# A gate-scaled one-hot matrix made by compare-then-multiply on VectorE, without ScalarE

## The chip, the cores and the metric

The kernel runs on one core of one Trainium2 chip. The core has five engines, each with a queue of its own that it works off in order: TensorE (PE in the profile, with PEld for its weight loads), VectorE (DVE), ScalarE (ACT), GpSimd (POOL) and SyncE (SP, which issues most DMAs). The metric is the device time of one execution in microseconds (us), the median of several runs.

## The reference: what is computed

The program is one layer of a hybrid decoder: a state-space branch, a dilated attention branch and a memory attention branch over 1024 tokens of width 1024, merged and added to the residual. Behind them stands a retrieval layer (PEER), and the change lies there. For each token, 8 heads choose 16 experts each out of 16384 = 128 x 128, so a token has 128 chosen experts with a softmax gate each:

```python
idx = jnp.take_along_axis(cidx, pos, axis=-1)
gate = jax.nn.softmax(top, axis=-1)
u = expert_down[ib]
act = jax.nn.gelu(jnp.einsum('bld,blhkd->blhk', hb, u), approximate=False)
coef = (gb * act.astype(F32)).astype(hb.dtype)
vv = expert_up[ib]
return jnp.einsum('blhk,blhkd->bld', coef, vv)
```

## The kernel before

The 1024 tokens are 8 tiles of 128. Four of them (`GATHERED`: 0, 1, 4, 5) fetch the rows of the chosen experts one by one: GpSimd gathers a row per token, VectorE takes its dot product with the token (L1109), and TensorE sums the rows of the second table (L1154). The other four (`DENSE`: 2, 3, 6, 7) compute all 16384 experts with matmuls and multiply the result by a matrix W of gates that is zero for an expert that a token did not choose. W is parked in HBM as `w_park` and read back as `wbig` tiles in the dense part.

`gates_of` builds W, four tokens in a step, 32 steps for a tile. An expert's number is split into a high part (number >> 7) and a low part. The two parts and the gate are transposed, so that `sl[:, n, t]` holds for token t, on partition j, what its j-th choice has: n = 0 the high part, n = 1 the low part, n = 2 the gate. For the four tokens of a step, VectorE compares a row of 0 to 127 (`iota`) with the low parts (`o2`, L1221) and with the high parts (`og`, L1222), each as one operation of 128x512. ScalarE multiplies each token's 128x128 block of `og` by that token's gates (L1224, four operations). In `product`, one step later, TensorE multiplies the two blocks for each token (L172, four matmuls of 128x128, held in program order by `pinned`), and ScalarE copies the result from PSUM into a stage tile (L1207), which SP writes to `w_park` after every four steps (L1210).

Two stretches of the program run this. The first does tiles 2 and 3 as a side job (`early_gates`) beside the front part of the second half: there `og` and `o2` are `work` tiles and the PSUM tile is called `s`. The second does tiles 6 and 7 (`gates` in `dense`) beside `begin`, which computes 23 slices of the dense hidden layer ahead, each with 24 matmuls, two ScalarE casts (`whi`, L244) and two VectorE subtractions (`wlo`, L245). There the one-hot tiles lie in a `wbig` buffer (`hots`, four steps deep) and the PSUM tile is called `mm`; `coef` is the name of the tile that holds `sl`. Beside both, VectorE does the dot products of the gathers (L1109) and the choice of experts (`top16` and `two_heads`, L965 to L1008). After the second stretch come five more slices of the hidden layer, pinned behind it, and then the dense products of the remaining program.

The order of the work is set by the order in which the generators are advanced (by a running estimate of TensorE time), and then by the tile framework's scheduler, which sorts each engine's queue by priority and by its own idea of when an operand is ready. So a change of an operation's kind and engine can also move its neighbours.

Of the kernel before, what the change touches and what calls it, by code (L numbers as in the profile page):

```python
# [14 lines left out]
AF = mybir.ActivationFunctionType  # L15
ALU = mybir.AluOpType
# [86 lines left out]
def tile_hybrid_block(ctx: ExitStack, tc: tile.TileContext, keep_d, cst_d, vec_d, row_d, pos_d, xT_d, memT_d, w_in, w_mem_kv,  # L103
                      w_ssd_br, w_dil_br, w_mem_br, w_out, w_query, subk_d, down_d, up_d, downT_d, out):
    nc = tc.nc
# [44 lines left out]
    def gtiny(n, dt, tag, bufs):  # L150
        return new(gsmall, [P, n], dt, tag, bufs)[:, :n]
# [8 lines left out]
    def ps(tag=None):  # L160
        turn[0] += 1
        return bank(tag if tag and psums[tag][1] else "t" if turn[0] % 2 and psums["t"][1] else "s")
# [7 lines left out]
    def mm(o, lhsT, rhs, **kw):  # L170
        cost(o, 4 if rhs.dtype == F32 else 1)
        return nc.tensor.matmul(o, lhsT, rhs, **kw)  # L172

    def tr(o, x, i):
        cost(o, 2)
        nc.tensor.transpose(o, x, i)  # L176
# [6 lines left out]
    iota = keep[:, K_IOTA:K_IOTA + P]  # L183
# [914 lines left out]
    def pinned(ins):  # L1098

        tc.keep_in_program_order(ins)  # L1100
# [83 lines left out]
    def gates_of(d, expert, gate, alloc, ps, hot, stage_of):  # L1184

        t, slots = alloc(), alloc()
        ei = gtiny(P, I32, "ei", 1)
        nc.vector.tensor_copy(ei, expert)
        nc.vector.tensor_scalar(out=ei, in0=ei, scalar1=7, scalar2=None, op0=ALU.logical_shift_right)
        nc.vector.tensor_copy(t[:, 0:128], ei)  # L1190
        nc.vector.scalar_tensor_tensor(t[:, 128:256], t[:, 0:128], -128.0, expert, op0=ALU.mult, op1=ALU.add)
        tp = ps()
        for n, x in enumerate((t[:, 0:128], t[:, 128:256], gate)):
            tr(tp[:, n * P:(n + 1) * P], x, ident)
        nc.scalar.copy(slots[:, 0:384], tp[:, 0:384])
        yield
        sl = slots[:, 0:384].rearrange("p (n t) -> p n t", n=3)
        iota4 = iota.unsqueeze(1).to_broadcast([P, 4, P])
        todo = []

        def product():
            (o2, og), stage, b, t4 = todo.pop(0)
            pw = ps()
            for tq in range(4):
                pinned(mm(pw[:, tq * P:(tq + 1) * P], o2[:, tq, :], og[:, tq, :], start=True, stop=True))
            for c0, n, part in stage:
                nc.scalar.copy(part[:, :, t4 * 4:t4 * 4 + 4], pw.rearrange("p (t c) -> p c t", t=4)[:, c0:c0 + n, :])  # L1207
            if t4 == WT // 4 - 1:
                for c0, n, part in stage:
                    nc.sync.dma_start(w_park[d * (P // WT) + b, :, c0:c0 + n, :], part)  # L1210

        for b in range(P // WT):
            stage = stage_of(b)
            for t4 in range(WT // 4):
                t0 = b * WT + t4 * 4

                def of(n):
                    return sl[:, n, t0:t0 + 4].unsqueeze(2).to_broadcast([P, 4, P])

                o2, og = (hot(n).rearrange("p (t c) -> p t c", t=4) for n in range(2))  # L1220
                nc.vector.tensor_tensor(out=o2, in0=iota4, in1=of(1), op=ALU.is_equal)  # L1221
                nc.vector.tensor_tensor(out=og, in0=iota4, in1=of(0), op=ALU.is_equal)  # L1222
                for tq in range(4):
                    nc.scalar.activation(out=og[:, tq, :], in_=og[:, tq, :], func=AF.Copy, scale=sl[:, 2, t0 + tq:t0 + tq + 1])  # L1224
                todo.append(((o2, og), stage, b, t4))
                if len(todo) == 2:
                    product()
                yield
        product()

    def dense(hn, dpool):
# [54 lines left out]
        def gates():  # L1286
            stages = new(dpool, [P, 2, P, WT], F32, "wbig", 2)
            hots = new(dpool, [P, 8, NW], F32, "wbig", 2)
            step = [0]

            def hot(n):
                step[0] += n == 0
                return hots[:, 2 * (step[0] % 4) + n, :]

            for d, tt in enumerate(DENSE):
                if tt >= NT:
                    while tt not in routed:
                        next(sides[-1][0])
                        yield
                    yield from gates_of(d, *routed[tt], dslab, big_ps, hot, lambda b: [(0, P, stages[:, b % 2])])  # L1300
# [92 lines left out]
    def early_gates():  # L1393
        def stage_of(b):
            return [(32 * k, 32, work().rearrange("p (c t) -> p c t", t=WT)) for k in range(4)]

        for d, tt in enumerate(DENSE):
            if tt < NT:
                while tt not in routed:
                    yield IDLE  # L1400
                for _ in gates_of(d, *routed[tt], work, ps, lambda n: work(), stage_of):
                    yield paces["gates"]
# [90 lines left out]
```

## Time and profile before

| | us |
|---|---|
| median of 3 runs | 4039.79 |
| lowest and highest run | 4023.14, 4045.42 |
| the profiled execution, its own time | 4024.51 |
| its span, first to last instruction | 4022.6 |
| first stretch of gate steps (tiles 2 and 3) | 1666 to 2042 |
| second stretch of gate steps (tiles 6 and 7) | 2236 to 2411 |

The profile shows one execution. An engine is busy while an instruction of it runs; instructions of one engine overlap a little, so the distance from one start to the next is what an instruction takes from its queue, and its duration is longer. The idle time of an engine is put down to what it waited for last. PE is the busiest engine over the span, and the stretches differ: the table of stretches further down gives the busy time of each engine in each.

### The profile page before, as it was taken

How to read it: one execution, taken by the hardware profiler on the slowest of the kernel's cores; microseconds unless marked ns; L12 is line 12 of the kernel's file. 1: busy time of each engine (PE TensorE's matmuls, PEld its weight loads, DVE VectorE, ACT ScalarE, POOL GpSimd, SP SyncE). 2: the span in 40 equal slices, each digit the busy share in tenths (PEclk: the TensorE clock that was granted, in tenths of full speed). 3: DMA queues.
4: the chain of work that ended last, by engine and by line, in shares of the span. 5: the costliest groups of instructions: out<-in, count | busy, mean ns of one | idle time of the engine just before them, and what ended most of it. 6: DMA issues, size and time to landing. Idle time of an engine off the chain costs nothing.

```text
span 4022.6 us, 54006 instructions
## 1 busy us (share of the span) xinstructions
PE 3743.0 (93%) x17838; PEld 2805.3 (70%) x17838; DVE 2759.6 (69%) x7131; ACT 1502.5 (37%) x3326; POOL 1200.8 (30%) x1081
## 2 busy tenths in 40 slices
PE   8989999999989998898898888989999999999997
PEld 5766888877766786666566665667777777777664
DVE  5763454559988768898769997876667666666432
ACT  4543344343533333455542682222223222222221
POOL 0000000000123323344344323434443345444444
PEclk9989999999999988999999998999999999999999
DMA  3233233444556756788788878989998889889898
GB/s 96 75 96 90 76 108 110 137 148 136 152 173 211 231 172 229 256 312 303 278 321 313 308 259 298 317 273 318 318 319 291 290 306 324 304 310 314 302 323 312
DMA packets 452824, 956.28 MB, mean 238 GB/s; under 512 B 44480, under 2 KB 173248, under 8 KB 450496
## 3 DMA queue, kind: packets, MB, share of 16 engines
q0 software_dynamic: 147456, 536.94, 38.3%
q1 hardware_dynamic: 305088, 415.90, 31.9%
q8 instruction: 140, 2.29, 0.2%
q14 instruction: 140, 1.15, 0.1%
HBM read 882.94 MB, written 69.73 MB: 237 GB/s over the span
## 4 chain that ended last, share of the span: by engine, by line
PE 62%; DMA 13%; DVE 12%; issue 8%; POOL 2%; ACT 2%; SPq 0%; POOLq 0%; DVEq 0%; ACTq 0%
PE mm L172 36%; PE s L172 18%; PE up L1154 4%; DMA wraw<-in_downT_dram 3%; PE t L172 3%; DMA rowd<-in_down_dram,ids 3%; DVE rowd L1109 2%; DVE wlo L245 2%; DMA wraw<-in_up_dram 2%; POOL rowd L1115 1%; PE s L176 1%; DMA rowd<-in_up_dram,ids 1%; DMA slab<-y_park 1%; DMA rowu<-in_up_dram,ids 1%; DVE junk L1007 1%
## 5 line engine op out<-in xcount | busy, mean ns | idle before, releaser
L244 ACT CAST whi<-wraw 128x512 fp32r<-128x512 f32 (+2 forms) x1002 | 613.6, 613 | 1701.3 <-PE mm L172 775.7
L245 DVE TENSOR_TENSOR wlo<-wraw,whi 128x512 fp32r<-128x512 f32 (+2 forms) x1002 | 678.3, 679 | 763.3 <-ACT whi L244 671.1
L1115 POOL DMA_INDIRECT rowd<-in_down_dram,ids x512 | 603.5, 1179 | 1227.2 <-DVE act L1109 809.6
L172 PE MATMUL mm<-uslab,whi 128*128 128x512 f32 x2240 | 735.3, 406 | 0.3 <-ACT uslab L244 0.2
L172 PE MATMUL mm<-whi,coef 128*128 128x512 f32 x2048 | 677.6, 401 | 32.1 <-DVE acc L1345 17.1
L172 PE MATMUL s<-uslab,whi 128*128 128x512 f32 (+1 forms) x2080 | 664.2, 401 | 36.3 <-ACT whi L244 29.1
L1109 DVE CUSTOM_DVE_ANT_0 rowd<-rowd,rowd 128x1024 f32<-128x1024 f32 x512 | 616.9, 1219 | 111.3 <-DMA rowd<-in_down_dram,ids 107.2
L1168 POOL DMA_INDIRECT rowu<-in_up_dram,ids x448 | 514.7, 1149 | 575.5 <-PE up L1154 452.8
L172 PEld LDWEIGHTS s<-uslab,whi 128*128 128x128 f32 (+1 forms) x2080 | 390.2, 190 | 164.0 <-issue 37.4
L172 PEld LDWEIGHTS mm<-whi,coef 128*128 128x128 f32 x2048 | 389.8, 190 | 156.7 <-issue 45.4
L172 PEld LDWEIGHTS mm<-uslab,whi 128*128 128x128 f32 x2240 | 419.7, 192 | 93.6 <-issue 10.8
L172 PE MATMUL mm<-uslab,wlo 128*128 128x512 f32 x1120 | 450.5, 405 | 11.1 <-DVE wlo L245 10.9
L172 PE MATMUL s<-uslab,wlo 128*128 128x512 f32 (+1 forms) x1040 | 414.6, 399 | 8.4 <-DVE wlo L245 8.4
L172 PE MATMUL mm<-wlo,coef 128*128 128x512 f32 x1024 | 408.3, 399 | 0.0
L172 PE MATMUL mm<-slab,whi 128*128 128x512 f32 x768 | 253.6, 408 | 21.0 <-DVE slab L245 8.7
L172 PEld LDWEIGHTS mm<-uslab,wlo 128*128 128x128 f32 x1120 | 213.8, 191 | 63.0 <-DVE wlo L245 14.1
L1154 PE MATMUL up<-rowu,one_col 128*32 128x512 f32 x1792 | 225.5, 613 | 20.2 <-DMA rowu<-in_up_dram,ids 19.7
L527 POOL COPY slab<-halo 128x3 f32<-128x3 f32 x32 | 12.2, 385 | 766.6 <-DVE posf L1002 750.1
L172 PEld LDWEIGHTS s<-uslab,wlo 128*128 128x128 f32 (+1 forms) x1040 | 197.3, 190 | 60.4 <-DVE wlo L245 15.7
L172 PE MATMUL mm<-whi,uslab 128*128 128x512 f32 (+1 forms) x768 | 236.1, 388 | 0.0
L172 PEld LDWEIGHTS mm<-wlo,coef 128*128 128x128 f32 x1024 | 195.3, 191 | 46.8 <-issue 1.7
L172 PEld LDWEIGHTS mm<-slab,whi 128*128 128x128 f32 x768 | 143.1, 191 | 61.8 <-DVE slab L245 12.9
(314 smaller groups left out, 5035.8 us busy)
## 6 DMA issues: line engine op xcount, KB each, us to landing
wraw<-in_downT_dram SPq DMA_DIRECT2D x256, 256.0 KB
wraw<-in_up_dram SPq DMA_DIRECT2D x256, 256.0 KB
wraw<-in_w_in_dram SPq DMA_DIRECT2D x152, 256.0 KB
wbig<-w_park SPq DMA_DIRECT2D x16, 2048.0 KB
wraw<-in_w_in_dram SPq DMA_DIRECT2D x160, 128.0 KB
slab<-y_park SPq DMA_DIRECT2D x64, 256.0 KB
wraw<-in_w_query_dram SPq DMA_DIRECT2D x64, 256.0 KB
w_park<-work SPq DMA_DIRECT2D x64, 256.0 KB
```

The costliest lines, as they stand in the source:

```text
L172: return nc.tensor.matmul(o, lhsT, rhs, **kw)
L176: nc.tensor.transpose(o, x, i)
L244: nc.scalar.copy(hi, src)
L245: nc.vector.tensor_tensor(out=lo, in0=src, in1=hi.bitcast(F32), op=ALU.subtract)
L527: nc.gpsimd.tensor_copy(r[:, 0:3], halo[:, f, :])
L1007: nc.vector.tensor_tensor(out=junk, in0=junk, in1=d3[:, h, :].unsqueeze(1).to_broadcast([P, 16, NCAND]), op=ALU.mult)
L1109: pinned(nc.vector.tensor_tensor_reduce(out=r, in0=r, in1=hn, scale=1.0, scalar=0.0, op0=ALU.mult, op1=ALU.add, accum_out=act[:, j:j + 1]))
L1115: nc.gpsimd.indirect_dma_start(out=r, out_offset=None, in_=down_d, in_offset=bass.IndirectOffsetOnAxis(ap=ids[:, j:j + 1], axis=0))
L1154: pinned(nc.tensor.matmul(up[32 * q:32 * q + 32, hh * 512:(hh + 1) * 512], z[:, q, 31 - n:63 - n], four[q][:, hh * 512:(hh + 1) * 512], st ...
L1168: nc.gpsimd.indirect_dma_start(out=r, out_offset=None, in_=up_d, in_offset=bass.IndirectOffsetOnAxis(ap=ids[:, 128 + t:129 + t], axis=0))
```

## The change

The compare of the high part is no longer made for four tokens at once and then scaled on ScalarE. For each token, one VectorE operation takes `iota`, compares it with the token's high parts (one value for each partition) and multiplies the outcome by the token's gates (again one value for each partition).

```diff
                 nc.vector.tensor_tensor(out=o2, in0=iota4, in1=of(1), op=ALU.is_equal)
-                nc.vector.tensor_tensor(out=og, in0=iota4, in1=of(0), op=ALU.is_equal)
                 for tq in range(4):
-                    nc.scalar.activation(out=og[:, tq, :], in_=og[:, tq, :], func=AF.Copy, scale=sl[:, 2, t0 + tq:t0 + tq + 1])
+                    nc.vector.tensor_scalar(out=og[:, tq, :], in0=iota, scalar1=sl[:, 0, t0 + tq:t0 + tq + 1],
+                                            scalar2=sl[:, 2, t0 + tq:t0 + tq + 1], op0=ALU.is_equal, op1=ALU.mult)
```

Over the program this takes 512 operations of 128x128 from ScalarE and 128 of 128x512 from VectorE, and adds 512 of 128x128 to VectorE.

The end of VectorE's queue in the second stretch, before (rows without numbers at their start; `keep` holds `iota`, `top` and `cand` belong to the choice of experts, `wlo` to the hidden layer):

```order
L1221 TENSOR_TENSOR wbig_19631<-keep,coef_21666 128x512
L966 MAX_INDEX pos_22183<-top_21057,cand_22127 128x8
L1222 TENSOR_TENSOR wbig_19631<-keep,coef_21666 128x512
L967 MATCH_REPLACE cand_22127<-top_21057,cand_22127 128x50
L245 TENSOR_TENSOR wlo_22257<-wraw_22254,whi_22256 128x512
L968 MAX top_21057<-cand_22127 128x8
L245 TENSOR_TENSOR wlo_22275<-wraw_22272,whi_22274 128x512
```

The same place in the changed kernel:

```order
L1221 TENSOR_TENSOR wbig_19567<-keep,coef_21570 128x512
L966 MAX_INDEX pos_22059<-top_20977,cand_22006 128x8
L1223 TENSOR_SCALAR wbig_19567<-keep,coef_21570 128x128
L967 MATCH_REPLACE cand_22006<-top_20977,cand_22006 128x50
L1223 TENSOR_SCALAR wbig_19567<-keep,coef_21570 128x128
L968 MAX top_20977<-cand_22006 128x8
L1223 TENSOR_SCALAR wbig_19567<-keep,coef_21570 128x128
L969 MAX_INDEX pos_22059<-top_20977,cand_22006 128x8
L1223 TENSOR_SCALAR wbig_19567<-keep,coef_21570 128x128
L245 TENSOR_TENSOR wlo_22129<-wraw_22126,whi_22128 128x512
L245 TENSOR_TENSOR wlo_22147<-wraw_22144,whi_22146 128x512
```

One operation of a step has become four, and the small operations that stood between the steps now stand between the four as well. Between the first and the last gate operation of this stretch the queue holds the same other work in both kernels, but for one pass of `top16` whose last pieces cross the end (27 against 28 of L967 to L969).

The end of ScalarE's queue in the second stretch, before:

```order
L1207 COPY wbig_19630<-mm_22223 128x128x4
L1224 ACTIVATE wbig_19631<-wbig_19631,coef_21666 128x128 x4
L1207 COPY wbig_19630<-mm_22240 128x128x4
L1207 COPY wbig_19630<-mm_22246 128x128x4
L1075 ACT_TABLE_LOAD
```

And in the changed kernel:

```order
L1207 COPY wbig_19566<-mm_22096 128x128x4
L1207 COPY wbig_19566<-mm_22112 128x128x4
L1207 COPY wbig_19566<-mm_22118 128x128x4
L244 CAST whi_22196<-wraw_22194 128x512
L1075 ACT_TABLE_LOAD
```

Nothing but the copies out of PSUM is left of the gate steps on ScalarE.

VectorE's queue in the first stretch, at the 18th step, before (`rowd` is a gathered row, `slab` and `wlo` belong to the front part):

```order
L1221 TENSOR_TENSOR work_15872<-keep,work_14893 128x512
L966 MAX_INDEX idxs_15795<-vals_15794,sc_15792 128x8
L1222 TENSOR_TENSOR work_15873<-keep,work_14893 128x512
L245 TENSOR_TENSOR slab_15836<-slab_15710,slab_15835 128x512
L967 MATCH_REPLACE sc_15792<-vals_15794,sc_15792 128x128
```

And in the changed kernel:

```order
L1221 TENSOR_TENSOR work_15855<-keep,work_14893 128x512
L966 MAX_INDEX idxs_15779<-vals_15778,sc_15776 128x8
L1223 TENSOR_SCALAR work_15856<-keep,work_14893 128x128
L967 MATCH_REPLACE sc_15776<-vals_15778,sc_15776 128x128
L1223 TENSOR_SCALAR work_15856<-keep,work_14893 128x128
L968 MAX vals_15778<-sc_15776 128x8
L1223 TENSOR_SCALAR work_15856<-keep,work_14893 128x128
L969 MAX_INDEX idxs_15779<-vals_15778,sc_15776 128x8
L1109 ISA rowd_15666,act_13895<-rowd_15666,rowd_13893 128x1024
L1109 ISA act_13895 128x1
L1223 TENSOR_SCALAR work_15856<-keep,work_14893 128x128
```

Here the fourth token's operation has come to stand behind a dot product of a gathered row. The order of TensorE's matmuls moves by a few places in both stretches, and the last matmul of the second stretch keeps its place among the others.

## Rows read from the trace of the kernel before

**Rows 1.** Busy time and share of the span of each engine, from the page.

```profile
PE 3743.0 (93%) x17838; PEld 2805.3 (70%) x17838; DVE 2759.6 (69%) x7131; ACT 1502.5 (37%) x3326; POOL 1200.8 (30%) x1081
```

**Rows 2.** Busy time by stretch: stretch, its length, then each engine's busy us.

```profile
core 0: us, PE busy (x) PEld busy (x) DVE busy (x) ACT busy (x) POOL busy (x), PEclk, DMA share, GB/s
1666.00:1850.00 184.00, 161.98 (x852) 120.94 (x851) 157.92 (x424) 98.82 (x324) 71.99 (x63) 0.97 0.88 308
1850.00:2042.00 192.00, 165.35 (x859) 117.02 (x859) 138.87 (x249) 111.14 (x343) 79.76 (x66) 0.96 0.82 296
2160.00:2236.00 76.00, 68.21 (x305) 49.09 (x298) 74.50 (x296) 21.51 (x36) 35.11 (x28) 0.96 0.85 301
2236.00:2408.00 172.00, 152.80 (x895) 121.48 (x893) 167.13 (x538) 129.31 (x353) 52.27 (x38) 0.99 0.78 281
2408.00:2600.00 192.00, 165.50 (x731) 120.54 (x732) 154.87 (x423) 51.18 (x90) 76.70 (x63) 0.92 0.89 304
2600.00:3700.00 1100.00, 1063.71 (x4918) 794.34 (x4917) 724.45 (x1283) 308.72 (x518) 481.97 (x420) 0.98 0.89 306
```

**Rows 3.** Groups by line and shape: count, busy us, mean ns, idle before and releasers.

```profile
L172 PE MATMUL s<-work,work 128*128 128x128 f32 x576 | 84.8, 288 | 17.7 <-ACT work L1224 15.2 <-DVE work L890 2.3
L172 PE MATMUL mm<-wbig 128*128 128x128 f32 x512 | 78.0, 300 | 16.9 <-ACT wbig L1224 15.6 <-issue 1.1
L1224 ACT ACTIVATE wbig<-wbig,coef 128x128 f32<-128x128 f32 x256 | 82.2, 395 | 10.1 <-DVE wbig L1222 9.2 <-ACT whi L244 0.6
L1222 DVE TENSOR_TENSOR wbig<-keep,coef 128x512 f32<-128x512 f32 x64 | 43.6, 681 | 0.0
```

**Rows 4.** Timeline of the second stretch's last steps: start us, duration us, engine, operation.

```profile
2388.39 0.68 DVE L1221 TENSOR_TENSOR wbig<-keep,coef 128x512 f32<-128x512 f32 x1
2388.98 0.69 DVE L1222 TENSOR_TENSOR wbig<-keep,coef 128x512 f32<-128x512 f32 x1
2389.58 0.29 DVE L965 MAX8 vals<-sc 128x8 f32<-128x128 f32 x1
...
2388.58 1.29 ACT L1224 ACTIVATE wbig<-wbig,coef 128x128 f32<-128x128 f32 x4
2389.76 0.58 ACT L1207 COPY wbig<-mm 128x512 f32<-128x512 f32 x1
2390.22 1.30 ACT L1224 ACTIVATE wbig<-wbig,coef 128x128 f32<-128x128 f32 x4
...
2407.30 0.67 DVE L1222 TENSOR_TENSOR wbig<-keep,coef 128x512 f32<-128x512 f32 x1
...
2409.76 1.37 PE L172 MATMUL mm<-wbig 128*128 128x128 f32 x8 [0.28 <-ACT wbig L1224]
2410.89 0.71 PE L172 MATMUL s<-uslab,whi 128*128 128x512 f32 x2
```

**Rows 5.** VectorE's timeline around operations of 128x128.

```profile
2347.59 0.21 DVE L1189 TENSOR_SCALAR ei<-ei 128x128 int32<-128x128 int32 x1
2347.71 0.09 DVE L967 MATCH_VALUE_LOAD sc<-vals,sc 128x8 f32 x1
...
2348.31 0.28 DVE L1191 SCALAR_TENSOR_TENSOR coef<-coef,expert 128x128 f32<-128x128 f32 x1
2348.50 0.09 DVE L969 MATCH_VALUE_LOAD idxs<-vals,sc 128x8 f32 x1
...
84.38 0.60 DVE L600 SCALAR_TENSOR_TENSOR work<-slab,vec,s 128x128 f32<-128x128 f32 x2
```

**Rows 6.** VectorE groups by line and shape, as in rows 3.

```profile
L600 DVE SCALAR_TENSOR_TENSOR work<-slab,vec,s 128x128 f32<-128x128 f32 x32 | 9.6, 342 | 0.0
L503 DVE SCALAR_TENSOR_TENSOR tiny<-tiny,tiny 128x64 f32<-128x64 f32 x16 | 3.5, 218 | 0.3
L361 DVE TENSOR_SCALAR tiny<-tiny 128x64 f32<-128x64 f32 x1 | 0.2, 195 | 0.0
```

**Rows 7.** Timeline of one step of the first stretch.

```profile
1742.11 0.68 DVE L1222 TENSOR_TENSOR work<-keep,work 128x512 f32<-128x512 f32 x1
...
1742.88 0.40 ACT L1224 ACTIVATE work<-work,work 128x128 f32<-128x128 f32 x1 [6.25 <-DVE work L1222]
...
1743.33 0.49 PE L172 MATMUL s<-work,work 128*128 128x128 f32 x2 [1.73 <-ACT work L1224]
```

**Rows 8.** Durations by line, ns min/median/max: a VectorE copy, a gather's issue on GpSimd.

```profile
L1151 DVE COPY one_col<-coefT x128: 148/168/347, 1582.4 to 4004.6; 128x4 f32<-128x4 f32 x128
L1115 POOL DMA_INDIRECT rowd<-in_down_dram,ids x512: 932/1026/3783, 1062.0 to 3737.7; - x171
```

## The prediction

> **What bounds the kernel now.** I read the shares first, then the stretches, then the groups and the timeline of the gate steps. Over the span TensorE is the busiest engine with 93% [rows 1]. The stretches say more [rows 2]. In the long dense part, 2600 to 3700, TensorE is busy for 1063.71 of 1100 us and VectorE for 724.45: what arrives later there ends later, and nothing makes it up. In the first stretch of gate steps (1666 to 2042) TensorE works 327.3 of 376 us (161.98 + 165.35), VectorE 296.8 and ScalarE 210.0: each has gaps, VectorE 79 us of them. In the second stretch (2236 to 2408) it is different: VectorE is busy for 167.13 of 172 us, TensorE for 152.80, ScalarE for 129.31. VectorE was as full from 2160 on (74.50 of 76). So in the second stretch VectorE's queue sets the pace, although the view of the groups blames ScalarE: TensorE's idle time before the gate matmuls is put down to the scaling, L1224, with 15.6 us in the second stretch and 15.2 us in the first [rows 3]. Both are true. ScalarE is the last link of each step, and behind it stands a VectorE that hasn't rested.
>
> The reader should see in the timeline [rows 4] what a step costs each engine near the end of the second stretch. VectorE starts `o2` at 2388.39, `og` at 2388.98 and the next operation at 2389.58: 0.60 us of its queue for each. ScalarE goes from one group of four scalings to the next in 1.64 us (2388.58 to 2390.22), of which the scalings take 1.18 (2388.58 to 2389.76). TensorE's eight passes take 1.37 us and then wait 0.28. The last `og` starts at 2407.30 and ends at 2407.97; the last gate matmuls are over when TensorE goes on with the hidden layer at 2410.89.
>
> **What is removed.** ScalarE loses 512 scalings. In the second stretch that is 64 x 1.18 = 75 us of its queue, and the 129 us of busy time fall to about 50 of 172 [rows 2, 4]. By itself this ends nothing earlier but the tail: after the last `og` TensorE needs 2.9 us today (2407.97 to 2410.89), the scaling between them. With the scaling gone it needs about 0.4, the matmuls of the last token: a gain of 2.5 us. VectorE loses 64 compares of 0.60 us in each stretch.
>
> **What is added.** Each step gets four operations of 128x128 with one input and two values for each partition. No row shows that form, so I bound its place in the queue, start to start. The same kind of operation with constants in the place of the values, L1189, takes 0.12 us (2347.59 to 2347.71) [rows 5]; that is the low end. What a value for each partition costs is seen between two operations of 128x128 with two inputs: without one, L1191 takes 0.19 us (2348.31 to 2348.50); with one, L600 takes 0.26 (two have a joint extent of 0.60 and a mean duration of 0.342, so their starts are 0.26 apart) [rows 5, 6]. So a value costs 0.07. If the fetch of the second hides behind that of the first, the new operation takes 0.12 + 0.07 = 0.19; if they come one after the other, 0.26. The high end is an operation that runs as slowly as one with two inputs, 0.19 + 0.14 = 0.33. Against that high end speaks that a one-input compare-and-multiply in f32 of 64 columns (L361) took 195 ns where a two-input one (L503) took 218 [rows 6]: the one-input form does go faster, with two steps too. I take 0.21, near the hidden fetch: L600's price is a fixed delay before the data flow, and two such delays can overlap.
>
> A step of `og` then costs VectorE 4 x 0.21 = 0.84 us in place of 0.60: 0.24 more, and 64 x 0.24 = 15.4 us in each stretch.
>
> **The second stretch.** The order shows the same other work in VectorE's queue between the first and the last gate operation, and no later work is pulled in. So the last gate operation moves by 15.4 us less what VectorE's idle time of 4.9 us (172 less 167.13) gives back. Some of that idle time is waiting for a ScalarE that will be freer; I take 2 us. With the 2.5 us of the tail: 15.4 - 2 - 2.5 = +11 us. TensorE's last gate matmul stands at the same place in its queue, the five hidden slices are pinned behind it, and the dense part follows. That TensorE no longer waits for L1224 is no gain here, since it will wait for VectorE in its place.
>
> **The first stretch.** The step in [rows 7] shows the chain: `og` starts at 1742.11, the first scaling at 1742.88, TensorE at 1743.33, 1.22 us after the compare began. With the change TensorE can start behind the first of the four, about 0.3 us after it began, so such a gap closes by some 0.9 us. The 15.2 us that TensorE waits for L1224 there make room for about six such gaps: -5 us. Against it stand 15.4 us more on VectorE, which has 79 us of gaps; if a third of it falls where VectorE is late, that is +5. The order also puts a fourth operation behind a dot product here and there. I count nothing for this stretch, with 5 us to either side (10 at the high price).
>
> **The sum.** +11 us. On the profiled execution that is 4024.51 + 11 = 4035.5. That execution lies 15.3 us under the median of the runs, at their low end, so I put the same difference on the median: 4039.79 + 11 = 4051.
>
> **A rule that speaks against the change.** L1151 is a VectorE copy with one input in SBUF. Its 128 instances run while GpSimd issues gathers of about 1.03 us each, and the longest took 347 ns [rows 8]. The Trainium skill, "SBUF — State Buffer", § SBUF: two separate sides, says that a VectorE operation in a two-port mode and a GpSimd operation exclude each other for a whole instruction. By that rule each new operation that comes upon a gather would stand until it is over; by the row, none of 128 stood longer than 0.2 us.
>
> **The rivals.**
>
> *The scaling was the link that counted.* If the new operation costs no more than 0.15 us, a step takes no more of VectorE than before, and the waits for L1224 go. At 0.12 the second stretch gains 64 x (0.60 - 0.48) = 8, the tail 2.5 and up to 2 more of idle time, and the first stretch loses most of its 15 us of waits: about -26, 4014 us. For it speaks the 31 us of waits in [rows 3]; against it the price of a value in [rows 5], which decides.
>
> *The new operation is dear, and the kernel is slower.* The mechanism is the same queue, VectorE in the second stretch; it decides from 0.25 us on. At 0.26 a step grows by 0.44 and the stretch by 28 - 4.5 = 23.5 us, with 5 for the first stretch +28: 4068. At 0.33 a step grows by 0.72, the stretch by 46 - 4.5 = 41, with up to 10 for the first +51: 4091. For it speaks that a step brings four operations in place of one and each pays its fixed part; against it only the one-input speed in [rows 6].
>
> *GpSimd and the new operation exclude each other.* GpSimd is busy for 52.27 of 172 us in the second stretch [rows 2], so 30% of 256 operations would meet a gather and wait half of it, 0.5 us: 256 x 0.30 x 0.5 = 38 us on top of the 11. That gives 4089. Against it stands the copy in [rows 8].
>
> *Nothing is left at the end.* After the second stretch TensorE idles 26.5 us (192 less 165.50) between 2408 and 2600 [rows 2]. If those gaps shrink because loads that TensorE waits for there have been issued at the old time, the 11 us are taken back: 4040. Against it, the loads go by buffers that the same late matmuls free.
>
> **How the numbers follow.** Half a per cent, 20 us, is about what a measurement of this kernel can tell from no change. My forecast, 4051, has 0.45; the taken-back lengthening, 4040, 0.18; the gain, 4014, 0.08; the dear operation, 4068 to 4091, 0.25; the exclusion, 4089, 0.04. Faster by over 0.5% (under 4020) is the gain and a little scatter: 0.09. Slower (over 4060) is the exclusion, most of the dear operation and a bit of the forecast's own upper side: 0.30. The rest is 0.61. The range leaves out the gain, the exclusion and the upper half of the dear operation: 4024 to 4075.
>
> **What would show it.** Right: L1223's starts about 0.21 us apart; VectorE without gaps in the second stretch and ScalarE at about 50 us; the last gate matmul over some 11 us later, measured from the first gate operation; TensorE's waits there put down to L1223. Wrong: a start-to-start of 0.15 or less, or of 0.25 or more; single L1223 of over 0.5 us beside gathers; VectorE idle in the second stretch, which would mean that something else holds it; a first stretch that moves by more than 10 us either way; or a later start of the dense part whose delay is gone at 2600.

## The result, and the profile after

| | before | after |
|---|---|---|
| median of the runs, us | 4029.72 (six, 4017.59 to 4045.42) | 4055.47 (six, 4050.40 to 4059.18) |
| profiled execution, us | 4024.51 | 4055.87 |

The ratio is 1.0062, with a 95% interval of 1.0040 to 1.0085: the change costs about 25 us (16 to 34), just over the half per cent that a measurement of this kernel can tell. The prediction said +11 us. The absolute 4051 is closer to 4055 than that, but by luck: it stood on a median of three runs of before, and with more runs of before that median is 10 us lower. What has to be explained is +25 where +11 was forecast; both lie inside the range.

Where the 31 us between the two profiled executions lie is seen from the starts of the first compare and the ends of the last gate operations in both traces:

| stretch | before, us | after, us | difference |
|---|---|---|---|
| start of the span to the first compare | 1666.1 | 1668.3 | +2.2 |
| first stretch: first compare to the end of the last `og` | 371.6 | 377.5 | +5.9 |
| between | 198.6 | 201.3 | +2.7 |
| second stretch: first compare to the end of the last gate matmul | 174.8 | 198.3 | +23.5 |
| from there to the end of the span | 1611.5 | 1608.6 | -2.9 |

How far one profile can be off is seen in the kernels of the experiments below that leave a stretch as it is: the first stretch took 371.6 to 375.2 us in them, the second 174.8 to 178.1, and the first compare came at 1659.7 to 1671.2. So only the second stretch has a difference that one pair of profiles can show, and it is 20 to 23.5 us.

The page's line of busy times, which answers to [rows 1]. VectorE has 384 instructions more, ScalarE 512 fewer:

```profile
PE 3759.8 (93%) x17838; PEld 2816.1 (69%) x17838; DVE 2811.5 (69%) x7515; ACT 1358.3 (34%) x2814; POOL 1205.0 (30%) x1081
```

VectorE's busy time grew by 52 us (2759.6 to 2811.5) and ScalarE's fell by 144 (1502.5 to 1358.3), and the kernel is slower. The windows, with the columns of [rows 2], show the four stretches of after:

```profile
1668.00:2046.00 378.00, 327.95 (x1672) 239.25 (x1670) 315.35 (x852) 134.35 (x404) 148.27 (x124) 0.93 0.82 290
2247.00:2445.00 198.00, 163.92 (x912) 128.18 (x911) 194.76 (x735) 59.72 (x105) 48.54 (x38) 0.91 0.69 249
2445.00:2620.00 175.00, 150.71 (x662) 110.08 (x662) 140.71 (x366) 44.63 (x74) 67.25 (x57) 0.93 0.92 310
2620.00:3730.00 1110.00, 1073.53 (x4953) 801.84 (x4952) 734.89 (x1329) 311.82 (x523) 495.94 (x425) 0.98 0.88 306
```

In the second stretch VectorE is busy for 194.76 of 198 us while ScalarE's time has fallen to 59.72. VectorE still sets the pace there, and the stretch is longer by what VectorE was given. The groups answer to [rows 3]:

```profile
L172 PE MATMUL s<-work,work 128*128 128x128 f32 x576 | 86.1, 290 | 14.1 <-DVE work L1223 9.4 <-DVE work L890 2.9 <-ACT work L1207 0.9
L172 PE MATMUL mm<-wbig 128*128 128x128 f32 x512 | 78.3, 305 | 12.4 <-DVE wbig L1223 10.9 <-ACT wbig L1207 1.5
L1223 DVE TENSOR_SCALAR work<-keep,work 128x128 f32<-128x128 f32 x256 | 76.5, 347 | 2.4 <-DMA w_park<-work 2.3
L1223 DVE TENSOR_SCALAR wbig<-keep,coef 128x128 f32<-128x128 f32 x256 | 74.9, 337 | 0.0
```

TensorE's waits for the scaling (15.2 and 15.6 us) became waits for the new operation (9.4 and 10.9). The timeline of the last steps, which answers to [rows 4], shows the price that counts, that from start to start:

```profile
2439.25 0.67 DVE L1221 TENSOR_TENSOR wbig<-keep,coef 128x512 f32<-128x512 f32 x1
2439.84 1.10 DVE L1223 TENSOR_SCALAR wbig<-keep,coef 128x128 f32<-128x128 f32 x4
2440.32 1.16 PE L172 MATMUL mm<-wbig 128*128 128x128 f32 x8 [0.64 <-DVE wbig L1223]
2440.86 0.68 DVE L1221 TENSOR_TENSOR wbig<-keep,coef 128x512 f32<-128x512 f32 x1
...
2444.63 0.33 DVE L1223 TENSOR_SCALAR wbig<-keep,coef 128x128 f32<-128x128 f32 x1
2444.88 1.29 DVE L245 TENSOR_TENSOR wlo<-wraw,whi 128x512 fp32r<-128x512 f32 x2
2445.26 0.71 PE L172 MATMUL s<-uslab,whi 128*128 128x512 f32 x2
```

Four new operations hold VectorE from 2439.84 to 2440.86: 1.02 us, 0.256 each. The prediction took 0.84 for the four. After the last of them (2444.63 + 0.33 = 2444.96) TensorE goes on with the hidden layer 0.3 us later, where it needed 2.9 before: the tail went as forecast.

### The profile page after: what moved, and what is told of

Read it like the earlier page. It is cut to its first block, busy times and chain, and to the rows that moved or that the text cites. A ratio compares the mean times of both kernels' runs of the same rounds, so it can differ in the third digit from the quotient of the medians.

```text
span 4054.1 us, 53856 instructions
## 1 busy us (share of the span) xinstructions
PE 3759.8 (93%) x17838; PEld 2816.1 (69%) x17838; DVE 2811.5 (69%) x7515; ACT 1358.3 (34%) x2814; POOL 1205.0 (30%) x1081
## 4 chain that ended last, share of the span: by engine, by line
PE 63%; DMA 14%; DVE 12%; issue 7%; POOL 2%; ACT 1%; SPq 0%; POOLq 0%; ACTq 0%; DVEq 0%
PE mm L172 37%; PE s L172 17%; DMA wraw<-in_downT_dram 5%; PE up L1154 4%; PE t L172 3%; DMA wraw<-in_up_dram 2%; DVE rowd L1109 2%; DVE wlo L245 2%; DMA rowd<-in_down_dram,ids 2%; DMA slab<-y_park 1%; DVE wbig L1223 1%; POOL rowd L1115 1%; DMA rowd<-in_up_dram,ids 1%; PE s L176 1%; DMA rowu<-in_up_dram,ids 1%
## 5 line engine op out<-in xcount | busy, mean ns | idle before, releaser
L1109 DVE CUSTOM_DVE_ANT_0 rowd<-rowd,rowd 128x1024 f32<-128x1024 f32 x512 | 616.6, 1217 | 99.2 <-DMA rowd<-in_down_dram,ids 98.7
```

The lines of the kernel that those rows point to most:

```text
L1109: pinned(nc.vector.tensor_tensor_reduce(out=r, in0=r, in1=hn, scale=1.0, scalar=0.0, op0=ALU.mult, op1=ALU.add, accum_out=act[:, j:j + 1]))
```

## The experiments

Each ratio is to the kernel before, run beside it on the same chip. Where nothing else is said, the diffs are against the changed kernel.

### Each stretch alone

The diff is that of e1_first; e2_second has `if d >= 2`.

```diff
+                if d < 2:
                     for tq in range(4):
                         nc.vector.tensor_scalar(out=og[:, tq, :], in0=iota, scalar1=sl[:, 0, t0 + tq:t0 + tq + 1],
                                                 scalar2=sl[:, 2, t0 + tq:t0 + tq + 1], op0=ALU.is_equal, op1=ALU.mult)
+                else:
+                    nc.vector.tensor_tensor(out=og, in0=iota4, in1=of(0), op=ALU.is_equal)
+                    for tq in range(4):
+                        nc.scalar.activation(out=og[:, tq, :], in_=og[:, tq, :], func=AF.Copy, scale=sl[:, 2, t0 + tq:t0 + tq + 1])
```

> The new form in the first stretch of gate steps alone (tiles 2 and 3); the second stretch as before. Theory (VectorE's queue in the second stretch sets the pace, and a new operation costs 0.256 us of it): the first stretch has gaps on VectorE that hide most of it; the changed kernel's trace has this stretch 6 us longer than before's. So 3 to 10 us slower than before, and the second stretch keeps its 174.8 us from its first compare to its last gate matmul. Rival (the first stretch is the cause, by fourth operations that stand behind dot products): 15 us slower or more. Rival (ScalarE's relief is a gain there): faster than before.

> The new form in the second stretch alone (tiles 6 and 7); the first as before. Theory: 64 x (4 x 0.256 - 0.60) = 27 us more on VectorE's queue, less 2 to 4 us for the shorter tail and VectorE's idle time: the stretch from its first compare to its last gate matmul goes from 174.8 to about 198 us, and the time is 20 to 27 us over before. Rival (the first stretch is the cause): under 10 us over before.

The first stretch alone: 1.0032 (1.0015 to 1.0049), 13 us (6 to 20). The second alone: 1.0039 (1.0022 to 1.0056), 16 us (9 to 23). Both lie outside what was expected (3 to 10, and 20 to 27), with intervals that reach into it. Together that is 29, which agrees with the whole change's 25 (16 to 34). So by the times the new form in the first stretch, which the prediction put at nothing, carries about half. The profile doesn't show where: with the first stretch alone this stretch takes 374.3 us, no more than in kernels that leave it alone, and that execution was the fastest of the kernel's twelve runs. The second alone, in its window:

```profile
2240.00:2437.00 197.00, 162.03 (x909) 126.92 (x908) 194.75 (x734) 60.32 (x106) 47.59 (x38) 0.91 0.70 247
```

VectorE is as full as in after, and the stretch takes 196.9 us (174.8 before). That is 22 us more for a kernel that is 16 slower; the paragraph "Nothing is left at the end" below comes back to it.

### What a value for each partition costs

```diff
-                                            scalar2=sl[:, 2, t0 + tq:t0 + tq + 1], op0=ALU.is_equal, op1=ALU.mult)
+                                            scalar2=0.5, op0=ALU.is_equal, op1=ALU.mult)
```

(e4_one; in e3_const the first value is a constant too, `scalar1=5.0`.)

> As the changed kernel, but both values of each new operation are constants (5.0 and 0.5) in place of values for each partition; the matrix of gates is then not the right one, all else is done. Theory (the two fetches are the price): starts 0.12 to 0.13 us apart, a step's four take 0.50 us in place of the 0.60 of the old compare, the second stretch is 64 x 0.1 = 6 us shorter on VectorE and 2.5 us in the tail: 165 to 172 us there, and the time 5 to 20 us under before. Rival (four operations in place of one are what costs, or GpSimd's exclusion, or the changed order): starts 0.19 us apart or more, and no faster than before.

> As the changed kernel, but only the compared value is one for each partition, and the gate is the constant 0.5 (the matrix of gates is then not the right one). Theory (each value costs 0.067 us, one after the other): starts 0.19 us apart, 64 x (0.76 - 0.60) = 10 us more on VectorE's queue in the second stretch, less 4: about 181 us there, and the time about midway between the kernel with constants and the changed one, 0 to 10 us over before. Rival (the first value costs it all, the second nothing): starts 0.256 us apart, as slow as the changed kernel.

The groups of the second stretch, two constants first:

```profile
L1223 DVE TENSOR_SCALAR wbig<-keep 128x128 f32<-128x128 f32 x256 | 44.7, 222 | 0.0
```

```profile
L1223 DVE TENSOR_SCALAR wbig<-keep,coef 128x128 f32<-128x128 f32 x256 | 60.5, 281 | 0.0
```

With two values for each partition it was 337 ns (above): 222, 281, 337. From start to start the medians are 0.135, 0.196 and 0.256 us. Each value adds 0.06, the second as much as the first: no fetch hides behind the other. A run of four with constants:

```profile
2299.87 0.63 DVE L1223 TENSOR_SCALAR wbig<-keep 128x128 f32<-128x128 f32 x4
2300.41 0.21 DVE L965 MAX8 top<-cand 128x8 f32<-128x50 f32 x1
```

0.54 us for four, where the prediction's low end of 0.12 would make 0.48. The times are 0.9934 (0.9913 to 0.9955) with two constants, 26 us faster than before; 1.0000 (0.9982 to 1.0018) with one value; 1.0062 with two. VectorE's queue for `og` changes by 512 x 0.135 - 128 x 0.60 = -8 us, +24 and +54; the times by -26, 0 and +25. The three points lie on a line that rises by 0.82 us for each us of VectorE and stands at -20 where VectorE's load is unchanged. So there are two large terms: some 20 us that ScalarE's relief gives, and VectorE's load at nearly its full weight. And four operations in place of one are not in themselves what costs: with constants there are four as well, and the kernel is faster than before. One miss is left without a cause: with one value the second stretch took 191.2 us where 181 had been expected, though the kernel's time is where it was expected.

### The relief by itself

The diff is against the kernel before; e8_noscale1 keeps the loop, under `if d >= 2`.

```diff
                 nc.vector.tensor_tensor(out=og, in0=iota4, in1=of(0), op=ALU.is_equal)
-                for tq in range(4):
-                    nc.scalar.activation(out=og[:, tq, :], in_=og[:, tq, :], func=AF.Copy, scale=sl[:, 2, t0 + tq:t0 + tq + 1])
```

> The kernel before without the scaling on ScalarE: the one-hot matrices stay unscaled, so the matrix of gates is not the right one, and VectorE's work is unchanged. The three runs with the new operation at 0.135, 0.196 and 0.256 us lie on a line: -26, 0 and +25 us for -8, +24 and +54 us of VectorE's queue in both stretches together, slope 0.83, and -20 us where VectorE's work is unchanged. Theory now (the change has two halves that nearly cancel: ScalarE's relief is worth 20 us): about 20 us faster than before, 12 to 28. Rival, the prediction's view (VectorE is the pace in the second stretch and the relief is worth the tail and a few gaps): 2 to 8 us faster.

> The kernel before without the scaling on ScalarE in the first stretch alone (that half of the matrix of gates stays unscaled); VectorE's work is unchanged. With no scaling in both stretches the first one was 353.6 us long in place of 371.6 and the second 180.0 in place of 174.8. Theory (ScalarE's relief is worth 18 us, all of it in the first stretch, where work behind a waiting scaling stands in ScalarE's queue): 15 to 26 us faster than before. Rival (the relief comes from both stretches alike): 8 to 13 us faster.

Without any scaling: 0.9941 (0.9925 to 0.9958), 24 us less. Without it in the first stretch alone: 0.9960 (0.9947 to 0.9973), 16 us less. The line above said 20. The windows of the first of the two kernels:

```profile
1666.00:2020.00 354.00, 313.64 (x1657) 232.13 (x1656) 288.88 (x660) 132.74 (x399) 143.31 (x123) 0.95 0.87 311
2219.00:2399.00 180.00, 151.26 (x907) 120.57 (x906) 167.98 (x538) 59.87 (x107) 50.59 (x38) 0.94 0.76 270
```

The first stretch takes 353.6 us (355.8 in the other kernel) instead of 371.6: 16 to 18 less, beyond the scatter. The second takes 180.0 instead of 174.8, with VectorE's 167.98 us in place of 167.13 and ScalarE's 59.87 in place of 129.31: freeing ScalarE there didn't shorten it. The difference of 8 us between the two kernels' times has an uncertainty of its own size, so whether the second scaling gives anything at all stays open. The window shows nothing; behind it, from the last gate matmul to the end, the first kernel needs 1597.7 us and the other 1620.5.

### The load by itself

The diff is against the kernel before, and that of e6_twice2; e6_twice1 has `if d < 2`.

```diff
                 nc.vector.tensor_tensor(out=og, in0=iota4, in1=of(0), op=ALU.is_equal)
+                if d >= 2:
+                    nc.vector.tensor_tensor(out=og, in0=iota4, in1=of(0), op=ALU.is_equal)
```

> The kernel before with the compare of the high part made twice in the second stretch: 64 x 0.60 = 38 us more on VectorE there, ScalarE as before, result unchanged. Theory (VectorE's queue sets the pace there): the stretch goes from 174.8 to about 208 us and the time up by 28 to 36 us. Rival (ScalarE's last link sets the pace, VectorE runs ahead of it): up by under 15 us.

> The kernel before with the compare of the high part made twice in the first stretch: 38 us more on VectorE there, which has 79 us of gaps, ScalarE as before, result unchanged. The prediction's view (a third of it counts): up by 8 to 16 us. Rival (VectorE's load counts as fully in the first stretch as in the second, because its gaps are waits that come later too): up by 28 to 36 us.

64 compares more are 38 us of VectorE. In the second stretch they cost 33 us (1.0081, 1.0060 to 1.0101), in the first 43 (1.0107, 1.0087 to 1.0127), above even the rival's 28 to 36. The window of the first stretch with the extra compare:

```profile
1666.00:2077.00 411.00, 345.99 (x1700) 250.76 (x1698) 331.93 (x731) 211.42 (x658) 149.60 (x126) 0.90 0.78 274
```

VectorE is busy for 331.93 of 411 us, idle for 79. Before the change it was idle for 79 of 376 [rows 2]. The stretch takes 410.5 us instead of 371.6: the load was added, and the idle time stayed as it was. What VectorE waits for in that stretch, in the kernel before (total us, times, longest):

```profile
DVE rowd L1109 <- DMA rowd<-in_down_dram,ids: 24.6, 9, 7.0
DVE wlo L245 <- ACT whi L244: 22.4, 15, 4.8
DVE tiny L231 <- PE s L176: 9.3, 1, 9.3
```

and with the extra compare:

```profile
DVE wlo L245 <- ACT whi L244: 22.3, 19, 4.5
DVE rowd L1109 <- DMA rowd<-in_down_dram,ids: 20.4, 6, 6.5
DVE tiny L231 <- PE s L176: 7.8, 1, 7.8
```

The same three waits, of nearly the same size. The first is for gathers that GpSimd issues, and the page of after says what GpSimd waits for ahead of them, over the whole span:

```profile
L1115 POOL DMA_INDIRECT rowd<-in_down_dram,ids x512 | 599.8, 1171 | 1231.4 <-DVE act L1109 792.5
```

It waits for VectorE's own L1109. So a later VectorE makes later gathers, for which it then waits as long as before. A wait that moves along with the work offers no room. That the idle time didn't shrink is shown; that such loops are the reason is argued from these rows.

### Moving hidden work out of the second stretch

```diff
-D1, D2, D3, U1, U3, U4, H1, H3, L1, L2, L3, L4, WG = 2.31, 4.4, 4.4, 4.4, 4.4, 1.76, 3.0, 5.43, 9, 4.3, 2.52, 5, 4
+D1, D2, D3, U1, U3, U4, H1, H3, L1, L2, L3, L4, WG = 2.31, 4.4, 4.4, 4.4, 4.4, 1.76, 3.0, 5.43, 9, 4.3, 6, 5, 4
```

> The changed kernel with one number of the order changed (L3, the pace at which the choice of experts for tile 4 is advanced beside the second stretch, 2.52 to 6), which takes about 19 us of other work (four of eight passes of L1005 to L1008, fourteen of 28 of L965) out of VectorE's queue between the first and the last gate operation. Theory (VectorE's load in the second stretch): the stretch 15 to 19 us shorter than the changed kernel's 198.3, and the time 8 to 18 us under the changed kernel's, so 5 to 17 us over before. Rival (the work comes back later, because the gathers of tile 4 then start later): no faster than the changed kernel.

The second stretch did come down, from 198.3 us to 173.4, by 25 where 15 to 19 had been expected. The kernel takes 1.0145 (1.0124 to 1.0166): 58 us over before, so about 33 over the change. The work that no longer lies beside the gates comes at the end, as gathers and single-column products, with little else running. Its window:

```profile
3929.00:4105.00 176.00, 83.50 (x408) 16.34 (x400) 5.44 (x25) 0.00 (x0) 88.34 (x94) 0.63 0.83 295
```

From the last accumulation (`acc`) to VectorE's last operation the kernel needs 173 us here; the kernels before and after need 31 and 33. The theory had the direction of the stretch right and the rival had the time.

### The gates on ScalarE instead

VectorE's load counts in full, so I took it off VectorE. ScalarE makes a one-hot row alone: `abs(iota - high)` is 0 on the hit and at least 1 elsewhere, and `relu(gate - gate * abs)` is then the gate on the hit and 0 elsewhere. In e9_act1 this is done in the first stretch, in e10_acthalf in every other step of the second as well; the steps that are left are as in the kernel before. The diff is that of e9_act1; e10_acthalf has `if d < 2 or t4 % 2`.

```diff
+        ng = slots[:, 384:512]
+        nc.scalar.activation(out=ng, in_=tp[:, 256:384], func=AF.Copy, scale=-1.0)
...
+                if d < 2:
+                    for tq in range(4):
+                        col = t0 + tq
+                        nc.scalar.activation(out=og[:, tq, :], in_=iota, func=AF.Abs, scale=-1.0, bias=sl[:, 0, col:col + 1])
+                        nc.scalar.activation(out=og[:, tq, :], in_=og[:, tq, :], func=AF.Relu, scale=ng[:, col:col + 1], bias=sl[:, 2, col:col + 1])
```

> The other way round: in the first stretch ScalarE makes the gate-scaled matrix alone, two operations a token (the absolute difference of the row 0 to 127 and the high part, then gate minus gate times that, cut at zero), and VectorE makes only the compare of the low part; the second stretch as before; the result is the same matrix. VectorE loses 38 us in that stretch, ScalarE gains 75 us of work that no longer waits for VectorE. Theory (what counts in the first stretch is VectorE's load, about 1 us per us, and ScalarE's waiting behind VectorE): 25 to 50 us faster than before. Rival (ScalarE's longer work holds up its casts): no faster than before.

> As the kernel where ScalarE makes the matrix alone in the first stretch, and in the second stretch it does so in every other step: there VectorE loses 32 x 0.60 = 19 us of 167, and ScalarE gains 37 on 129, of 172. Theory: the second stretch goes from 174.8 to 158 to 168 us, and the time 7 to 17 us under that kernel's. Rival (ScalarE, then at 166 of 172, becomes the pace): the second stretch as long as before or longer.

1.0043 (1.0029 to 1.0057) and 1.0065 (1.0044 to 1.0085): 17 and 26 us slower than before. Both theories of a gain fell. The first kernel's groups, and the window of its first stretch:

```profile
L1228 ACT ACTIVATE work<-work,work 128x128 f32<-128x128 f32 x256 | 116.0, 495 | 0.0
L1227 ACT ACTIVATE work<-keep,work 128x128 f32<-128x128 f32 x256 | 91.2, 407 | 9.4 <-DMA h_park<-work 4.8 <-DMA w_park<-work 4.7
```

```profile
1662.00:2068.00 406.00, 342.51 (x1728) 251.50 (x1727) 262.64 (x611) 302.80 (x924) 150.69 (x133) 0.91 0.82 288
```

VectorE's 296.8 us fell to 262.64, ScalarE's 210.0 rose to 302.80, and the stretch went from 371.6 to 405.8, up to the last `og`, which ScalarE makes now (VectorE's last compare ends after 395.5). The second stretch then starts 591.6 us after the first compare, where it was 570.3. ScalarE is idle for 103 us of the stretch, and yet 93 us more on it made it 34 longer, with 34 us less on VectorE beside them. So the first stretch answers to load on ScalarE as it does to load on VectorE, although both have idle time. In the other kernel the second stretch takes 198.4 us with ScalarE busy for 177.78: there it has become as long as with the new operation, on another engine.

### The scaling one step later

The diff is against the kernel before; `late` is 1 in the first stretch and 0 in the second, and `scaled()` runs the loop over `tq` for the oldest of `fresh` and then appends its item to `todo`.

```diff
-                for tq in range(4):
-                    nc.scalar.activation(out=og[:, tq, :], in_=og[:, tq, :], func=AF.Copy, scale=sl[:, 2, t0 + tq:t0 + tq + 1])
-                todo.append(((o2, og), stage, b, t4))
+                fresh.append((og, t0, ((o2, og), stage, b, t4)))
+                if len(fresh) > late:
+                    scaled()
```

> The kernel before with the scaling written one step later in the first stretch (compare of a step, then the scaling of the step before it, then the product of the step before that); same work on every engine, two more work tiles in use. In the kernel before, ScalarE's idle time ahead of the scalings there was 41.8 us, put down to VectorE's compare. Theory (ScalarE's relief is worth 16 to 18 us in the first stretch because other work no longer stands behind a scaling that waits): most of those 41.8 us go, and the time is 8 to 18 us under before. Rival (the relief is ScalarE's 75 us of work itself, wherever it stands): within 5 us of before, or slower, since the tiles are held longer.

0.9975 (0.9961 to 0.9990): 10 us faster than before (4 to 16), the only complete version that beats both kernels, by less than the half per cent. The group of TensorE in the first stretch and that of the scaling:

```profile
L172 PE MATMUL s<-work,work 128*128 128x128 f32 x576 | 80.2, 284 | 5.0 <-DVE work L890 2.9 <-ACT work L1218 1.3 <-ACT work L942 0.7
L1218 ACT ACTIVATE work<-work,work 128x128 f32<-128x128 f32 x256 | 85.7, 399 | 39.8 <-DVE work L1231 36.5 <-issue 3.0
```

TensorE's waits for the scaling fell from 15.2 us [rows 3] to 1.3. ScalarE's own waits for the compare, which the theory wanted gone, are still 36.5 us. So the time is in the lower half of what the theory gave, but not by the route that it gave: the wait that went was TensorE's. The profiled execution of this kernel was its longest (4032.34), and its first stretch took 371.4 us, as before (371.6). A new wait shows there: VectorE stands 20.4 us, where it stood 6.8 before, until a work tile has been written out, since the tiles are held longer:

```profile
DVE work L1230 <- DMA w_park<-work: 9.7, 4, 3.9
DVE work L1231 <- DMA w_park<-work: 6.2, 3, 3.9
DVE work L1230 <- DMA h_park<-work: 4.5, 1, 4.5
```

So the profile doesn't show where the 10 us lie, and how much of the relief of 16 to 18 us is this chain and how much the time that ScalarE itself gets back stays open.

## Why the prediction had the direction and not the size

**VectorE's queue sets the second stretch: held.** The stretch grew by 23.5 us while ScalarE's work there halved (129.31 to 59.72), and with all scaling gone and VectorE unchanged it didn't shrink (180.0).

**The price of the new operation: this term was mis-sized.** 0.21 us was taken, between 0.19 for a hidden second fetch and 0.26 for fetches one after the other. Measured: 0.256. The reason given, that two fixed delays can overlap, is refuted by 0.135, 0.196 and 0.256. The rows themselves had said 0.12 + 2 x 0.07 = 0.26; the choice against it had no row. At that price the prediction's formula for the second stretch, worked out under the dear operation, gives 23.5 us, and the two traces show 23.5. That it fits to the tenth is luck, given profiles that differ by 3 us, but its other terms (idle time given back, tail) held within that. From the stretch to the whole it is less: 16 us (9 to 23) with this stretch alone.

**The first stretch at nothing: both its terms failed.** It was -5 for closed gaps and +5 for a third of the new load. Each was much larger. The relief is 16 to 18 us in the windows of the two kernels without scaling, not 5: the sum of the waits booked on L1224, cut down to six closed gaps, is only part of it. What the rest is isn't shown: VectorE's waits for ScalarE's casts there fell from 22.4 us to 15.5 and 17.0, but they were 18.6 in a kernel that leaves this stretch alone (e2_second). The load of 64 x (4 x 0.256 - 0.60) = 27 us counts in full, not by a third: the extra compares cost 43 us for 38. 27 less 17 is +10; the new form there alone cost 13 (6 to 20). At the right price the prediction had +5 for this stretch. That each term was several times too small is shown by the stretches and by the times; how far their sum lies from nothing is less sure, since the profiles have 374.3 and 377.5 us for 371.6 to 375.2.

**The sum as the runs have it.** Relief of both stretches -24 (e5_noscale), load 54 us on VectorE at 0.82 to 1.1 for each us, +44 to +59: +20 to +35. Measured +25. The forecast and the dear rival's low end (+28, made of 23.5 and 5) were both this mechanism; the second has the price and nearly the sum.

**The scaling was the link that counted: half right.** The gain that this rival wanted is real, and the kernel with two constants, at its price of 0.135, is 26 us faster, as the rival worked out for 0.12. Its condition on the price failed.

**GpSimd and the new operation exclude each other: refuted at its price.** The durations of L1223 in the changed kernel (ns, least, median, most):

```profile
L1223 DVE TENSOR_SCALAR work<-keep,work x256: 321/339/560, 1669.5 to 2045.5; 128x128 f32<-128x128 f32 x128
L1223 DVE TENSOR_SCALAR wbig<-keep,coef x256: 316/334/455, 2247.8 to 2444.6; 128x128 f32<-128x128 f32 x128
```

Of the 512, 178 lie for most of their time beside a gather's issue on GpSimd. Those take 356 ns in the mean and 560 at most; the other 334 take 335 and at most 349. The neighbour costs 0.02 us each, 4 us in all, where the rival had 38. By the rule of the Trainium skill, "SBUF — State Buffer", § SBUF: two separate sides, each of these would have stood until its gather was over, if the form runs in a two-port mode. No run shows in which mode it runs, so the trace refutes the rival's price and not the rule. Four, all beside a gather, do exceed the 0.5 us that the prediction named as a sign (up to 560 ns), so a neighbour can cost 0.2 us, but none stood for the 1 us of a gather's issue.

**Nothing is left at the end: refuted for the whole, but part of it is taken back.** From the last gate matmul to the end of the span it is 1608.6 us instead of 1611.5, within the scatter. The other kernels say more. The six whose second stretch is as before need 1611 to 1623 us for this part, the seven with another second stretch (without the one of the moved work) 1598 to 1609, in the mean 13 less; so it is on each of the three chips that ran kernels of both kinds. TensorE's waits for VectorE's `acc` in the 280 us behind the last gate matmul (total us, times, longest), in e1_first and in e2_second:

```profile
PE mm L172 <- DVE acc L1350: 17.3, 3, 12.6
PE mm L172 <- DVE acc L1350: 10.1, 4, 5.5
```

So what arrives later does not all end later, as the prediction's first paragraph had it, and the gaps that shrink are waits for VectorE and not for loads. Lateness alone isn't the cause: the part is as short in the kernels with constants and without scaling (1604.2 and 1597.7), whose second stretch is not or hardly longer. That cause stays open.

**What would show it.** Of the signs named there, three were seen: starts 0.25 us or more apart (a sign of being wrong), TensorE's waits on L1223, ScalarE at "about 50" (59.72). The last gate matmul came 23.5 us later and not 11. Another sign of being wrong, that the first stretch would move by more than 10 us, would not have been seen: it moved by 5.9 between the two profiles, hardly more than their scatter, and only the kernels with one part each showed the two large terms that cancel in it.

## What to carry to other kernels

An operation in a form that no row shows is priced by adding each operand's own cost in full; that they overlap needs a row too. Idle time of an in-order engine isn't room for more work: ask of each of its waits whether it would end at the same time if the engine came later, and if not, count the added load in full; here 38 us more made the first stretch 35 to 39 longer, with 79 us idle before and after. A term that looks like zero because two effects cancel should be written as both, each with its bounds, since each can be several times the sum.

## What the runs showed of the hardware

- On VectorE a one-input f32 operation of 128x128 holds the queue for 0.135 us with two constants, and 0.06 us more for each of its two values for each partition. Its duration in the profile (222, 281, 337 ns) is 0.08 to 0.09 us more than that, since the next operation starts before it ends.
- On ScalarE the activation of 128x128 took 495 ns with scale and bias both for each partition (Relu) and 407 with the bias alone (Abs); which part of the difference is the function's isn't shown.
- TensorE's granted clock in the second stretch fell from 0.99 of full speed to 0.91 with the change, and to 0.84 with the extra compare there (of the two levels, 1.2 and 2.4 GHz, a mix). In the changed kernel TensorE stood for 0.46 to 0.75 us ahead of each of the last six groups of eight gate matmuls, where it had stood for 0.28 [rows 4]. Its busy time for about as many matmuls rose from 152.80 to 163.92 us. With VectorE setting the pace it didn't decide the stretch's length in the changed kernel; with the extra compare, where VectorE was idle for 10 of 223 us and the stretch took 221.4 where 208 had been expected, it may have, and that is open:

```profile
2236.00:2459.00 223.00, 182.40 (x919) 144.37 (x920) 212.55 (x618) 137.64 (x364) 58.01 (x38) 0.84 0.63 224
```
